# A flow-matching layer on one core: the modulation's loads kept one half tile behind, the gates' minimum split off, eight scalings moved to ScalarE

## The chip, the cores and the metric

The kernel runs on one core of a Trainium2 chip. The metric is the device time of one execution in microseconds (us), lower is better; the time of a kernel is the median of its runs. A core has five engines, each with an instruction queue of its own: TensorE (PE in the profile; its weight loads are PEld), VectorE (DVE), ScalarE (ACT), GpSimd (POOL) and SyncE (SP, which here only issues DMA transfers). They work on SBUF, 128 partitions of on-chip memory, and TensorE writes its sums into PSUM, eight banks of 128x512 fp32.

## The reference

One layer of a backbone: 512 latent tokens `x` and 256 context tokens `ctx`, width 2048, everything in fp32.

```python
mx = silu(c) @ w_mod + b_mod                      # 6 x 2048: shifts, scales and gates
sh1, sc1, gt1, sh2, sc2, gt2 = split(mx, 6)
hx = rmsnorm(x, norm1_g) * (1 + sc1) + sh1        # the context likewise, with c_ctx
q, k, v, g, lf, lb, cb, cc, cx = split_proj(hx @ w_in)
la_f = log_sigmoid(lf @ w_gate_f + b_gate_f) / 16  # la_b likewise: per-channel forget gates
o = gla_bidir(q, k, v, la_f, la_b, s_f, s_b)       # 4 heads, from the context's final states
mix = concat(rmsnorm(o) * gla_g * silu(g), cb * conv_w3(cc * cx)) @ w_out
x = x + gt1 * mix
h2 = rmsnorm(x, norm2_g) * (1 + sc2) + sh2
x = x + gt2 * ((silu(h2 @ w_ffn_gate) * (h2 @ w_ffn_up)) @ w_ffn_down)   # hidden width 5632
return rmsnorm(x, final_g)
```

Three pieces matter here. The vectors gt1, sh2, sc2 and gt2 are four of the six parts of `silu(c) @ w_mod`, 64 rows of 128 numbers, each a dot product of length 2048. The forget gates are log-sigmoids, computed as min(z, 0) - ln(1 + exp(-|z|)). The second norm's output h2 is a scale and a shift per channel of the transposed activations.

## The kernel before

**Products.** Each fp32 product is three TensorE products of a faster type: an operand is cast into a high part (`whi`, by ScalarE, line 106), and the remainder (`wlo`, by VectorE, line 107) is its low part; `mm3` then does low by high, high by low and high by high. Weights come as pieces of 128x1024 (512 KB) that SP's queue loads (line 122) into a ring of four tiles named "raw"; whi and wlo have rings of three. A projection unit is one such piece: 8 times 3 matmuls of 128x512.

**The program's stages**, in order of time: first norm and the projections of k and v (to about 290 us); the context's gates and final states, woven with the projections of q of heads 0 and 1 (to about 342); the latent gates, woven with a g projection and the first conv unit (to 412); four heads of the linear attention, woven with the remaining projections (to about 760); the output product; the FFN's up and gate products, which follow a scheme of seven half-sized products per pair instead of eight; the FFN's down products; the last norm.

**Banks.** In the stages up to the heads, PSUM is five banks of a tag "g" (`bank`) and three of a tag "a" (`abank`). Projections accumulate in "a".

**The modulation.** The dot products with w_mod are spread over the stages from 290 to 754 us. `mod_some` (lines 379 to 405) is called once per woven step (`weave`, line 564) and takes on average 1.84 half tiles of 128x1024 of w_mod: it issues the load of one and lets VectorE multiply it with silu(c) and sum it (line 405, named CUSTOM_DVE_ANT_0 in the trace and ISA in the order). There are three ways, chosen by `behind[0]`. Where it is 0, as up to the heads, the load goes through SP's queue into the ring "raw" (`load_raw`), and the reduce is issued at once. Where it is 2, as in the heads (line 705), the reduce comes two half tiles later, and the load goes through POOL's queue: two of three into tiles of their own ("wm", line 393), the third into the ring "raw" (line 397). Ahead of such a load POOL copies one column of the newest cast weight into the tile (lines 392 and 396), which ties the load's time to that cast.

**The gates.** For a group of 128 tokens, `gate_rows` does two products of 33 rows into two banks, `pzs`, one per direction. `log_gates` (lines 489 to 497) takes them: ScalarE does |z| from the banks (line 493), then one exp and one ln over both (494, 495; each has a load of its function table ahead of it), and VectorE takes min(z, 0) from the banks and subtracts the logarithm in one instruction (497). The tile `lg` between them exists once. `do_gates` does this for four groups, with one bank of "g" and one of "a".

**The second norm.** `norm2_scale` scales the rows; `norm2_back` transposes them back on TensorE, 128x256 at a time, and applies scale and shift from PSUM: the even pieces on ScalarE (line 983), the odd ones on VectorE (line 980). The first half of the tokens (hf = 0) is done while the output product runs, the second (hf = 1) inside the first column group of the FFN.

**Order.** A scheduler sets each engine's order from the order of the code and the dependencies, except SP's from the output product on, which follows the code. Each engine works in that order, so an instruction that waits holds up those behind it.

Of the kernel before, what the change touches and what calls it, by code (L numbers as in the profile page):

```python
# [11 lines left out]
ALU = mybir.AluOpType  # L12
# [41 lines left out]
def tile_hybrid_block(  # L54
# [6 lines left out]
    nc = tc.nc  # L61
# [16 lines left out]
    def big(dtype=F32):  # L78
        return xpool.tile([P, SEQ], dtype, tag="t", name="big")

    def hbig(dtype=F32, name="hbig"):
        return xpool.tile([P, SEQ], dtype, tag="h", name=name, bufs=32)

    def bank(name="bank"):
        return pspool.tile([P, 512], F32, tag="g", name=name, bufs=5)

    def abank(name="abank"):
        return pspool.tile([P, 512], F32, tag="a", name=name, bufs=3)
# [4 lines left out]
    def mm(o, l, r, start, stop):  # L93
        nc.tensor.matmul(o, l, r, start=start, stop=stop, skip_group_check=True)  # L94
# [24 lines left out]
    def load_raw(src):  # L119
        n = src.shape[-1]  # L120
        r = wpool.tile([P, 1024], F32, tag="raw", name="raw", bufs=4)
        nc.sync.dma_start(r[:, :n], src)
        return r[:, :n]
# [11 lines left out]
    def tok(t, tt):  # L135
        return t[:, tt * P : tt * P + P]
# [200 lines left out]
    def gate_rows(pz, half, d, a):  # L337

        q = slice(64 * half, 64 * half + 33)
        mm(pz, lfT[q, a : a + P], gatet[q, d, :], True, True)  # L340
# [6 lines left out]
    for i in range(KD):  # L347
# [4 lines left out]
        if i % 4 == 3:  # L352
            pcs = mod_cols(wsh, i - 3, 4)
            for c in range(4):
                nc.vector.tensor_scalar(shs[:, i - 3 + c, 0:2], pcs[:, 2 * c : 2 * c + 2], col(C_BMOD + i - 3 + c),
                                        None, op0=ALU.add)
# [19 lines left out]
    nmod, owed = [0], [0.0]  # L376

    pend, behind, unit = [], [0], []

    def mod_some(n, last):  # L380


        owed[0] += 2 * n
        while owed[0] >= 1 and (pend or nmod[0] < 2 * last):
            owed[0] -= 1
            if nmod[0] < 2 * last:
                j, hf = divmod(nmod[0], 2)
                src = wm2[j][:, hf * 1024 : hf * 1024 + 1024]
                if behind[0] and nmod[0] % 3:
                    w = gp.tile([P, 1024], F32, tag="wm", name="wm", bufs=2)  # L390

                    nc.gpsimd.tensor_copy(w[:, 0:1], unit[0])
                    nc.gpsimd.dma_start(w, src)
                elif behind[0]:
                    w = wpool.tile([P, 1024], F32, tag="raw", name="raw", bufs=4)
                    nc.gpsimd.tensor_copy(w[:, 0:1], unit[0])
                    nc.gpsimd.dma_start(w, src)
                else:
                    w = load_raw(src)
                pend.append((j, hf, w))  # L400
                nmod[0] += 1
                if len(pend) <= behind[0]:
                    continue
            j, hf, w = pend.pop(0)
            nc.vector.tensor_tensor_reduce(  # L405
                out=w, in0=w, in1=cbc[:, hf * 1024 : hf * 1024 + 1024], scale=1.0, scalar=0.0,
                op0=ALU.mult, op1=ALU.add, accum_out=modacc[:, j, hf : hf + 1])
# [81 lines left out]
    def log_gates(pool, tag, pzs, las):  # L489

        t = pool.tile([P, 2, 512], F32, tag=tag, name="lg")
        for i in range(2):
            nc.scalar.activation(t[:, i, :], pzs[i], AF.Abs)
        nc.scalar.activation(t, t, AF.Exp, scale=-1.0)
        nc.scalar.activation(t, t, AF.Ln, bias=onecol)
        for i in range(2):
            nc.vector.scalar_tensor_tensor(las[i], pzs[i], 0.0, t[:, i, :], op0=ALU.min, op1=ALU.subtract)

    def proj_units(acc, wsrc, x, units=(0, 1), part=ALL):

        for n, u in enumerate(units):
            w = load_w(wsrc[u], 8)
            unit[:] = [w[0][:, 0, 0:1].bitcast(F32)]
            for k in range(8):
                mm3(acc[:, part], sl(w, ALL, k), sl(x[8 * u + k], ALL, part), n == 0 and k == 0, n == 1 and k == 7)
            yield
# [5 lines left out]
    def do_q(h):  # L512
        acc = abank("acc")
        yield from proj_units(acc, wq[h], hx)
        q_t[h] = big()
        nc.scalar.activation(q_t[h], acc, AF.Copy, scale=QSCALE)

    def do_ctx():
        kds = [[], []]
        las = []  # L520
        for d in range(2):
            pzs = [bank("pzs") for _ in range(NCT)]
            for tt in range(NCT):
                gate_rows(pzs[tt], tt, d, SEQ + tt * P)
            las.append([big() for _ in range(NCT)])
            log_gates(hcpool, "lg", pzs, las[d])
            yield
        for d in range(2):
            for tt in range(NCT):
                pz = bank("pz")  # L530
                whole = tt == d
                mm(pz, cstt[:, B_SUFF + d, :], las[d][tt], True, not whole)
                if whole:
                    mm(pz, one16, las[d][1 - tt], False, True)
                tag, bufs = (("sq0", 2), (("lfs", "tm")[tt], 1))[d]
                e = hcpool.tile([P, 512], F32, tag=tag, name="kdc", bufs=bufs)
                nc.scalar.activation(e, pz, AF.Exp)
                nc.vector.tensor_tensor(e, e, kc[tt], op=ALU.mult)
                kds[d].append(e)
            yield  # L540
        S0[:] = [xpool.tile([P, 2, DV], F32, tag="t", name="s0") for h in range(HEADS)]
        for d in range(2):
            for hp in range(2):
                pz = bank("pz")
                for hh in range(2):
                    h = 2 * hp + hh
                    for tt in range(NCT):
                        mm(pz[:, hh * DV : hh * DV + DV], tok(kds[d][tt], h), vc[tt][hp][:, hh * DV : hh * DV + DV],
                           hh == 0 and tt == 0, tt == 1)
                for hh in range(2):  # L550
                    nc.any.tensor_copy(S0[2 * hp + hh][:, d, :], pz[:, hh * DV : hh * DV + DV])
            yield
# [11 lines left out]
    def weave(stages, fill):  # L564

        for _ in stages:
            next(fill, None)
            mod_some(MOD_STEP, 64)
        for _ in fill:
            mod_some(MOD_STEP, 64)  # L570

    weave(do_ctx(), (None for g in (do_q(0), do_q(1)) for _ in g))


    msk = []
    for d in range(2):
        t = hbig()
        nc.gpsimd.memset(t, 0.0)
        msk.append(t)
    las = [[hbig() for tt in range(NX)] for d in range(2)]  # L580

    def do_gates():
        for tt in range(NX):
            pzs = [bank("pzs"), abank("pzs")]
            for d in range(2):
                gate_rows(pzs[d], d, d, tt * P)
            log_gates(hcpool, "lg", pzs, [las[0][tt], las[1][tt]])
            yield
# [92 lines left out]
    def do_conv(c):  # L681
# [17 lines left out]
        mix[8 + c] = y  # L699

    weave(do_gates(), (None for g in (do_g(0), do_conv(0)) for _ in g))
    es_hc.close()
    es_g = ExitStack()
    gp = es_g.enter_context(tc.tile_pool(name="gp", bufs=1, side="right"))
    behind[0] = 2
    for h in range(HEADS):
# [3 lines left out]
        if h + 2 < HEADS:  # L710
            fill.insert(0, do_q(h + 2))
        weave(do_gla(h), (None for g in fill for _ in g))
    mod_some(128, 64)
    mod_finish(0, 64)
    nc.vector.tensor_scalar(gsc2, modv[:, 32:48], 1.0, None, op0=ALU.add)
# [19 lines left out]
    def bank8(name="bank8"):  # L735
        return ps2.tile([P, 512], F32, tag="b", name=name)

    def row2k(name):
        return fpool.tile([P, NB], F32, tag="e", name=name, bufs=17)
# [226 lines left out]
    def norm2_back(hf, units):  # L966
        for u in units:
            pt = bank8("pt")
            dst = row2k("h2") if hf else big()
            dst = dst.rearrange("p (k t) -> p k t", k=2)  # L970
            for kk in range(2):
                k = 2 * u + kk
                for t in range(2):
                    nc.tensor.transpose(pt[:, (2 * kk + t) * P : (2 * kk + t) * P + P],
                                        xs[2 * hf + t, k // 4][:, k % 4 * P : k % 4 * P + P], ident)
            for kk in range(2):
                k = 2 * u + kk
                src = pt[:, kk * HALF : kk * HALF + HALF]
                if kk:
                    nc.vector.tensor_scalar(dst[:, kk, :], src, gsc2[:, k : k + 1], modv[:, 16 + k : 17 + k],  # L980
                                            op0=ALU.mult, op1=ALU.add)
                else:
                    nc.scalar.activation(dst[:, kk, :], src, AF.Identity, scale=gsc2[:, k : k + 1],
                                         bias=modv[:, 16 + k : 17 + k])
            raws[hf, u] = dst
# [364 lines left out]
```

## Time and profile before

| | |
|---|---|
| median of 3 runs | 2287.91 us (2285.56 to 2290.13) |
| profiled execution | 2285.08 us |
| its span on the core | 2283.3 us |
| mean granted clock of TensorE | 0.996 |
| TensorE busy | 2233.8 us (98%) |
| VectorE busy | 1657.4 us (73%) |
| ScalarE busy | 1003.3 us (44%) |
| POOL busy | 248.4 us (11%) |

The profile is one execution. The span is the time from the first to the last instruction; the device time of the same execution is 1.8 us longer. Matmuls are pipelined: one of 128x512 takes 0.39 us in a row of the timeline but the next starts 0.2265 us after it. A row of waits names the engine, the tile and line that waited, and after the arrow what came last of the things it waited for.

### The profile page before, as it was taken

How to read it: one execution, taken by the hardware profiler on the slowest of the kernel's cores; microseconds unless marked ns; L12 is line 12 of the kernel's file. 1: busy time of each engine (PE TensorE's matmuls, PEld its weight loads, DVE VectorE, ACT ScalarE, POOL GpSimd, SP SyncE). 2: the span in 40 equal slices, each digit the busy share in tenths (PEclk: the TensorE clock that was granted, in tenths of full speed). 3: DMA queues.
4: the chain of work that ended last, by engine and by line, in shares of the span. 5: the costliest groups of instructions: out<-in, count | busy, mean ns of one | idle time of the engine just before them, and what ended most of it. 6: DMA issues, size and time to landing. Idle time of an engine off the chain costs nothing.

```text
span 2283.3 us, 28033 instructions
## 1 busy us (share of the span) xinstructions
PE 2233.8 (98%) x10276; PEld 1785.8 (78%) x10276; DVE 1657.4 (73%) x2069; ACT 1003.3 (44%) x1354; POOL 248.4 (11%) x396
## 2 busy tenths in 40 slices
PE   8999998999999999999999999999999999999997
PEld 4765666887788887777888888888888888888886
DVE  3566165565768646899788779878887887787885
ACT  3423155333233434665554455444545544433343
POOL 2433100222323000100000000000000000000000
PEclk9999999999999999999999999999999999999999
DMA  9683466565677354523643454354335596756752
GB/s 328 218 278 132 148 220 199 197 223 203 239 238 254 117 191 168 204 74 122 210 148 117 160 179 157 130 171 165 136 139 205 203 338 208 242 198 203 258 168 100
DMA packets 163410, 433.16 MB, mean 190 GB/s; under 512 B 18022, under 2 KB 38790, under 8 KB 163144
## 3 DMA queue, kind: packets, MB, share of 16 engines
q1 hardware_dynamic: 128984, 331.20, 43.4%
q0 software_dynamic: 22416, 78.66, 9.8%
q10 hardware_dynamic: 11872, 21.52, 2.5%
q8 instruction: 81, 1.33, 0.2%
q14 instruction: 57, 0.47, 0.1%
HBM read 380.95 MB, written 50.35 MB: 189 GB/s over the span
## 4 chain that ended last, share of the span: by engine, by line
issue 56%; POOL 2%; PE 1%; DVE 1%; ACT 0%; DMA 0%; POOLq 0%; DVEq 0%; ACTq 0%
POOL opd L1070 2%; PE acc L94 1%; DVE wlo L107 0%; DVE ch L849 0%; ACT y L1217 0%; DMA out<-g 0%; DVE u L1023 0%; POOL xnd L1026 0%; ACT whi L106 0%; POOL hbig L962 0%; DVE hbig L1024 0%; DVE u L869 0%; POOLq L1070 0%; ACT acc L1208 0%; DVE g L1205 0%
## 5 line engine op out<-in xcount | busy, mean ns | idle before, releaser
L106 ACT CAST whi<-ch 128x1024 fp32r<-128x1024 f32 x335 | 353.1, 1055 | 407.5 <-PE acc L94 343.3
L107 DVE TENSOR_TENSOR wlo<-ch,whi 128x1024 fp32r<-128x1024 f32 x335 | 407.6, 1221 | 122.7 <-ACT whi L106 121.9
L106 ACT CAST whi<-raw 128x1024 fp32r<-128x1024 f32 x258 | 271.0, 1052 | 455.9 <-PE acc L94 287.9
L107 DVE TENSOR_TENSOR wlo<-raw,whi 128x1024 fp32r<-128x1024 f32 x258 | 316.2, 1226 | 197.6 <-ACT whi L106 191.6
L94 PE MATMUL acc<-hhl,whi 128*128 128x512 f32 x640 | 199.1, 392 | 0.0
L94 PE MATMUL acc<-hhi,wlo 128*128 128x512 f32 x320 | 133.0, 417 | 11.8 <-DVE wlo L107 5.6
L94 PEld LDWEIGHTS acc<-hhl,whi 128*128 128x128 f32 x640 | 120.2, 188 | 27.3 <-issue 2.5
L1070 POOL DMA_DIRECT2D opd<-ol x80 | 43.3, 541 | 880.2 <-DVE ol L107 880.0
L405 DVE CUSTOM_DVE_ANT_0 wm<-wm,cbc 128x1024 f32<-128x1024 f32 x66 | 80.6, 1224 | 79.4 <-DMA wm<-wm 78.5
L94 PE MATMUL acc<-wlo,a6h 128*128 128x512 f32 (+1 forms) x330 | 127.4, 386 | 1.2 <-DVE wlo L107 1.2
L94 PE MATMUL acc<-wlo,a0h 128*128 128x512 f32 x324 | 127.5, 394 | 0.8 <-DVE wlo L107 0.8
L94 PE MATMUL acc<-whi,a6l 128*128 128x512 f32 (+1 forms) x330 | 127.1, 387 | 0.3 <-DVE v L869 0.3
L94 PE MATMUL acc<-whi,a6h 128*128 128x512 f32 (+1 forms) x330 | 127.2, 386 | 0.0
L94 PE MATMUL acc<-hhl,wlo 128*128 128x512 f32 x320 | 126.5, 395 | 0.0
L94 PE MATMUL acc<-whi,a5h 128*128 128x512 f32 x324 | 126.3, 390 | 0.0
L94 PE MATMUL acc<-hlo,whi 128*128 128x512 f32 x320 | 126.1, 394 | 0.2 <-DVE hlo L112 0.2
L94 PE MATMUL acc<-whi,a0h 128*128 128x512 f32 x324 | 126.2, 390 | 0.0
L94 PE MATMUL acc<-whi,a5l 128*128 128x512 f32 x324 | 126.2, 389 | 0.0
L94 PE MATMUL acc<-wlo,a5h 128*128 128x512 f32 x324 | 126.1, 389 | 0.0
L94 PE MATMUL acc<-whi,a0l 128*128 128x512 f32 x324 | 126.0, 390 | 0.0
L94 PE MATMUL acc<-hhi,whi 128*128 128x512 f32 x320 | 125.7, 393 | 0.0
L405 DVE CUSTOM_DVE_ANT_0 raw<-raw,cbc 128x1024 f32<-128x1024 f32 x62 | 75.4, 1222 | 49.0 <-DMA raw<-wm 48.8
(334 smaller groups left out, 4986.0 us busy)
## 6 DMA issues: line engine op xcount, KB each, us to landing
raw<-wu SPq DMA_DIRECT2D x92, 512.0 KB, 4.3
ch<-wu SPq DMA_DIRECT2D x88, 512.0 KB, 3.8
wm<-wm POOLq DMA_DIRECT2D x66, 512.0 KB, 5.4
raw<-wd SPq DMA_DIRECT2D x50, 512.0 KB, 5.8
raw<-wc SPq DMA_DIRECT2D x48, 512.0 KB, 4.9
opd<-oh ACTq DMA_DIRECT2D x80, 256.0 KB, 3.5
opd<-ol POOLq DMA_DIRECT2D x80, 256.0 KB, 3.9
ch<-wd SPq DMA_DIRECT2D x38, 512.0 KB, 4.3
```

Source lines behind the costliest of these rows:

```text
L94: nc.tensor.matmul(o, l, r, start=start, stop=stop, skip_group_check=True)
L106: nc.scalar.copy(hi, src)
L107: (eng or nc.vector).tensor_tensor(lo, src, hi, op=ALU.subtract)
L405: nc.vector.tensor_tensor_reduce(out=w, in0=w, in1=cbc[:, hf * 1024 : hf * 1024 + 1024], scale=1.0, scalar=0.0, op0=ALU.mult, op1=ALU.add, ...
L1070: nc.gpsimd.dma_start(opd[j][i, 1].rearrange("p k t -> p (k t)"), lo.bitcast(F32))
```

## The change

Three edits. First, `behind[0]` is 1 from the context's states on: the half tiles of w_mod of that stage and of the gates now go through POOL's queue, all of them into the ring "raw" (the condition for the separate tiles is now `behind[0] > 1`), each with the copy of a column ahead of it, and each is reduced one half tile later. Second, `log_gates` takes the minimum right after |z|, as a VectorE instruction of its own from the bank into the result's tile, and subtracts the logarithm there later; `do_gates` takes both banks from the tag "g". Third, for the second half of the tokens, ScalarE applies scale and shift to the odd pieces too.

```diff
@@ mod_some
-                if behind[0] and nmod[0] % 3:
+                if behind[0] > 1 and nmod[0] % 3:
                     w = gp.tile([P, 1024], F32, tag="wm", name="wm", bufs=2)
 
                     nc.gpsimd.tensor_copy(w[:, 0:1], unit[0])
@@ log_gates
         t = pool.tile([P, 2, 512], F32, tag=tag, name="lg")
+
         for i in range(2):
             nc.scalar.activation(t[:, i, :], pzs[i], AF.Abs)
+            nc.vector.tensor_scalar(las[i], pzs[i], 0.0, None, op0=ALU.min)
         nc.scalar.activation(t, t, AF.Exp, scale=-1.0)
         nc.scalar.activation(t, t, AF.Ln, bias=onecol)
         for i in range(2):
-            nc.vector.scalar_tensor_tensor(las[i], pzs[i], 0.0, t[:, i, :], op0=ALU.min, op1=ALU.subtract)
+            nc.vector.tensor_tensor(las[i], las[i], t[:, i, :], op=ALU.subtract)
@@ after weave
+    behind[0] = 1
     weave(do_ctx(), (None for g in (do_q(0), do_q(1)) for _ in g))
@@ do_gates
-            pzs = [bank("pzs"), abank("pzs")]
+            pzs = [bank("pzs") for _ in range(2)]
@@ norm2_back
-                if kk:
+                if kk and not hf:
                     nc.vector.tensor_scalar(dst[:, kk, :], src, gsc2[:, k : k + 1], modv[:, 16 + k : 17 + k],
                                             op0=ALU.mult, op1=ALU.add)
                 else:
```

The order of the engines differs in two places, about 290 to 412 us and about 980 to 1080 us. Numbers behind a name tell tiles of one name apart; they are not the same in the two kernels.

VectorE at the first latent gate stage, before: four reduces (each with a row that reads the sum) stand ahead of line 497.

```order
L405 ISA raw_2870,modacc_76<-raw_2870,cbc_79 128x1024
L405 ISA modacc_76 128x1
L405 ISA raw_2906,modacc_76<-raw_2906,cbc_79 128x1024
...
L405 ISA raw_2909,modacc_76<-raw_2909,cbc_79 128x1024
...
L497 SCALAR_TENSOR_TENSOR hbig_2676<-pzs_2684,lg_2688 128x512
L497 SCALAR_TENSOR_TENSOR hbig_2680<-pzs_2685,lg_2688 128x512
L107 TENSOR_TENSOR wlo_2840<-raw_2837,whi_2839 128x1024
```

The same stage now (line 495 is the minimum, line 499 the subtract):

```order
L553 COPY s0_2636<-pz_2664 128x256
L405 ISA raw_2793,modacc_76<-raw_2793,cbc_79 128x1024
...
L107 TENSOR_TENSOR wlo_2816<-raw_2813,whi_2815 128x1024
L495 TENSOR_SCALAR hbig_2690<-pzs_2698 128x512
L405 ISA raw_2843,modacc_76<-raw_2843,cbc_79 128x1024
...
L495 TENSOR_SCALAR hbig_2694<-pzs_2699 128x512
L405 ISA raw_2847,modacc_76<-raw_2847,cbc_79 128x1024
...
L499 TENSOR_TENSOR hbig_2690<-hbig_2690,lg_2702 128x512
L499 TENSOR_TENSOR hbig_2694<-hbig_2694,lg_2702 128x512
L107 TENSOR_TENSOR wlo_2867<-raw_2864,whi_2866 128x1024
```

The minima stand between reduces, and nothing after them reads the banks.

VectorE at the last gate stage and the conv's first pieces, now:

```order
L107 TENSOR_TENSOR wlo_2946<-raw_2943,whi_2945 128x1024
L499 TENSOR_TENSOR hbig_2693<-hbig_2693,lg_2855 128x512
L499 TENSOR_TENSOR hbig_2697<-hbig_2697,lg_2855 128x512
L405 ISA raw_2939,modacc_76<-raw_2939,cbc_79 128x1024
...
L405 ISA raw_2973,modacc_76<-raw_2973,cbc_79 128x1024
...
L405 ISA raw_2977,modacc_76<-raw_2977,cbc_79 128x1024
...
L107 TENSOR_TENSOR wlo_2987<-raw_2984,whi_2986 128x1024
L405 ISA raw_3014,modacc_76<-raw_3014,cbc_79 128x1024
...
L107 TENSOR_TENSOR wlo_3021<-raw_3018,whi_3020 128x1024
```

Each remainder of a weight stands behind reduces of half tiles that the copies of POOL tie to the cast of the weight before.

ScalarE at the second half of the norm, before:

```order
L983 ACTIVATE h2_7567<-pt_7566,modv_77,gsc2_78 128x256
L983 ACTIVATE h2_7575<-pt_7574,modv_77,gsc2_78 128x256
L983 ACTIVATE h2_7601<-pt_7600,modv_77,gsc2_78 128x256
L983 ACTIVATE h2_7609<-pt_7608,modv_77,gsc2_78 128x256
L106 CAST whi_7709<-ch_7428 128x1024
L106 CAST whi_7736<-ch_7452 128x1024
L106 CAST a1h_7616<-s_7618 128x512
```

And now:

```order
L986 ACTIVATE h2_7608<-pt_7607,modv_77,gsc2_78 128x256 x2
L986 ACTIVATE h2_7616<-pt_7615,modv_77,gsc2_78 128x256 x2
L986 ACTIVATE h2_7642<-pt_7641,modv_77,gsc2_78 128x256 x2
L986 ACTIVATE h2_7650<-pt_7649,modv_77,gsc2_78 128x256 x2
...
L106 CAST a1h_7657<-s_7659 128x512
...
L986 ACTIVATE h2_7690<-pt_7689,modv_77,gsc2_78 128x256 x2
L106 CAST whi_7750<-ch_7469 128x1024
```

The first two casts of the weights that come next (whi_7709 and whi_7736) stood behind four scalings; now the first (whi_7750) stands behind twelve, and the second, further down, behind all sixteen.

## The prediction

> **What bounds the kernel now.** I read the page's first part, then TensorE's waits, then the timeline around the two longest of them, then the ends of what they wait for.
>
> ```profile
> PE 2233.8 (98%) x10276; PEld 1785.8 (78%) x10276; DVE 1657.4 (73%) x2069; ACT 1003.3 (44%) x1354; POOL 248.4 (11%) x396
> ...
> PE acc L94 <- DVE wlo L107: 10.4, 11, 2.9
> ...
> PE acc L94 <- DVE hbig L497: 5.5, 1, 5.5
> ...
> PE pzs L94 <- DVE hbig L497: 2.4, 1, 2.4
> ```
>
> TensorE is busy in 2233.8 of 2283.3 us, so 49.5 us can be won at most. Its longest single wait (engine, tile and line, then what it waits for; us in total, times, longest) is 5.5 us, for line 497, the last step of the gates. A second one, 2.4 us, waits for the same line. The timeline shows both in one place (start, duration, engine, line, tiles; in brackets the idle time ahead of it and what ended it).
>
> ```profile
> 346.72 1.15 ACT L495 ACTIVATE lg<-lg,cidt 128x1024 f32<-128x1024 f32 x1
> ...
> 353.17 1.23 DVE L405 CUSTOM_DVE_ANT_0 raw<-raw,cbc 128x1024 f32<-128x1024 f32 x1 [2.50 <-DMA raw<-wm]
> ...
> 354.76 1.12 PE L94 MATMUL pzs<-gatet,lfT 33*128 33x512 f32 x2
> 355.76 1.22 DVE L405 CUSTOM_DVE_ANT_0 raw<-raw,cbc 128x1024 f32<-128x1024 f32 x1 [1.36 <-DMA raw<-wm]
> 356.91 1.28 DVE L497 SCALAR_TENSOR_TENSOR hbig<-pzs,lg 128x512 f32<-128x512 f32 x2
> 358.25 1.90 PE L94 MATMUL pzs<-gatet,lfT 33*128 33x512 f32 x2 [2.37 <-DVE hbig L497]
> 358.31 1.08 ACT L493 ACTIVATE lg<-pzs 128x512 f32<-128x512 f32 x2 [9.14 <-DVE hbig L497]
> ...
> 364.25 1.29 DVE L497 SCALAR_TENSOR_TENSOR hbig<-pzs,lg 128x512 f32<-128x512 f32 x2 [2.17 <-ACT lg L495]
> 365.60 0.79 PE L94 MATMUL acc<-hhi,wlo 128*128 128x512 f32 x1 [5.45 <-DVE hbig L497]
> ...
> 368.32 0.57 PE L94 MATMUL acc<-hhi,wlo 128*128 128x512 f32 x1
> ...
> 355.00:360.00 5.00, 2.63 (x4) 0.39 (x3) 3.57 (x5) 1.67 (x3) 0.00 (x0) 0.85 0.68 207
> 360.00:365.00 5.00, 0.15 (x1) 0.00 (x0) 1.98 (x4) 4.94 (x5) 0.00 (x0) 0.50 0.59 206
> 365.00:370.00 5.00, 4.40 (x13) 3.52 (x14) 1.68 (x3) 4.96 (x7) 0.00 (x0) 0.63 0.35 113
> ```
>
> The first stage's logarithm is ready at 346.72 + 1.15 = 347.9, and line 497 starts at 356.91: ahead of it in VectorE's queue stand reduces (line 405) that wait for loads of w_mod (2.50 and 1.36 us idle). Line 497 is the last reader of the banks, so the gate products of the next stage, and then everything behind them on TensorE, wait for it. The last three rows (stretch, length, busy of PE, PEld, DVE, ACT, POOL, granted clock, DMA share, GB/s) show the price: TensorE almost still from 357 to 365.6, a clock of 0.50, and 0.63 after it.
>
> **What the gates part removes.** Idle 2.37 + 5.45 = 7.8 us. The two gate products took 1.90, where the pair at 354.76 took 1.12: 0.8 more. From 365.60 to 368.32 lie six starts of matmuls, 0.45 us apart, where 24 matmuls of a unit at full clock take 5.44 us, 0.2265 each: 1.4 us. Together 9.9 us. With the minimum taken right after the product, a bank is free after Abs (0.54) and a minimum of the kind of line 497 (0.68) at most, not after the whole chain of 7.3 us from 358.31 to 365.5. I count the 9.9 as gone. Kept in full, by a minimum that stands behind a late reduce as in the order printed above, is the other end.
>
> **What the one-behind part adds.** From 290 to 412 us some 30 half tiles leave SP's queue for POOL's. Each now costs a POOL copy out of the newest cast, a POOL issue, and a reduce one half tile later.
>
> ```profile
> L405 DVE CUSTOM_DVE_ANT_0 raw<-raw,cbc x30: 1215/1224/1229, 293.6 to 409.8; 128x1024 f32<-128x1024 f32 x30
> L107 DVE TENSOR_TENSOR wlo<-raw,whi x16: 1214/1222/1226, 284.5 to 402.4; 128x1024 fp32r<-128x1024 f32 x16
> L106 ACT CAST whi<-raw x16: 1036/1050/1062, 290.2 to 406.8; 128x1024 fp32r<-128x1024 f32 x16
> ...
> L396 POOL COPY raw<-whi x33: 177/191/1268, 403.6 to 754.0; 128x1 f32<-128x1 f32 x33
> ...
> DMA to landing us min/median/max: 4.0/5.9/8.9
> ...
> raw<-wm SPq DMA_DIRECT2D x29, 512.0 KB, 4.8
> raw<-wq SPq DMA_DIRECT2D x6, 512.0 KB, 4.1
> raw<-wc SPq DMA_DIRECT2D x6, 512.0 KB, 4.3
> ...
> raw<-wm POOLq DMA_DIRECT2D x1, 512.0 KB, 4.7
> ...
> DVE raw L405 <- DMA raw<-wm: 24.7, 12, 4.2
> ```
>
> (First rows: count, then least, median and largest ns, first and last start. The landing row is that of POOL's loads into the ring, line 397, in the heads' stage; the rows below it are the loads of 285 to 410 us, SP's and one of POOL's, with the median to landing. The last row is this stretch's wait of the reduces for their loads now.) Weight loads and half tiles share the ring of four. With about two half tiles per weight unit, a weight's load takes the place of a half tile of two units before. So there is a circle over two units: cast of a unit, copy, POOL load, reduce, load of the weight two units on, its cast: 0.19 + 5.0 + 1.22 + 4.3 + 1.05 = 11.8 us, or 5.9 per unit, where TensorE wants one each 5.44. Sixteen units in this stretch lose 16 x 0.45 = 7 us. For POOL's load I take 5.0, between its least (4.0) and its median (5.9) of the busier stage. With 4.0 and SP's 4.1 the circle is 10.6, under 10.88: nothing is lost. With 5.9 and 4.8 it is 13.2, or 6.6 per unit: 18 us.
>
> VectorE's order adds to it. In the conv's piece of the order above, wlo_2987 stands behind the reduces of raw_2973 and raw_2977, which are fetched only after whi_2945 is cast. From the end of that cast: two copies 0.4, landing at 5.4, two reduces to 7.8, wlo to 9.1. The unit before, whose wlo ends at 1.3 at the earliest, has TensorE busy to 6.8. That is a hole of up to 2.3 us; before, the reduce in that place waited for a load that nothing tied to the cast. Walking the whole new order with these durations, four units are met so (holes of 2.1, 2.8, 0.3, 3.1), and the context's state products lose 0.8: 9.1 us, within the ring's bounds of 0 and 18. The ring and the queue are the same late loads, so I take 9.1 once.
>
> A hole costs more than itself when the clock falls. These rows weigh it:
>
> ```profile
> 905.00:910.00 5.00, 3.17 (x13) 2.02 (x12) 2.59 (x3) 4.02 (x5) 0.00 (x0) 1.00 0.01 5
> ...
> 1000.00:1005.00 5.00, 2.81 (x10) 1.99 (x9) 5.00 (x8) 2.66 (x4) 0.00 (x0) 0.86 0.00 0
> 1005.00:1010.00 5.00, 5.00 (x19) 3.98 (x19) 4.46 (x6) 2.66 (x4) 0.00 (x0) 0.80 0.00 0
> ...
> 1003.44 0.69 PE L94 MATMUL acc<-whi,a1l 128*128 128x512 f32 x1 [2.19 <-DVE a1l L107]
> ```
>
> 1.83 us without work at 905 kept the clock at 1.00; 2.19 us at 1001 brought 0.86 and 0.80, and 9 slow matmuls, about 1.8 us. Of my holes two or three reach that length: 0 to 5.4 us more; I take 0.9, half of one. The Trainium skill (TensorE: Matmul & The Clock Gate, "What's actually happening") has the gate fall after an idle window of about 3.4 us; by that none of the new holes would slow anything, and the term would be 0. The row at 1001 does not agree: the clock fell after less.
>
> The twelve more VectorE instructions (six calls, two minima each, 0.68 at most; the subtract takes the place of line 497 at about the same size) are 8 us of VectorE in a stretch where it stands idle 24.7 us for loads: nothing for TensorE, and inside the walk. The 29 copies are 0.19 each on POOL, which does nothing (0.00) in the three stretches above: nothing. The Trainium skill (SBUF — State Buffer, "SBUF: two separate sides") says that VectorE with two SBUF inputs and GpSimd share a pair of ports which one holds for a whole instruction; the copies' 177 to 1268 ns agree, the largest being one reduce long. It could delay a load by up to 1.1 us, which lies in the ring's bounds.
>
> Gates together: -9.9 + 9.1 + 0.9 = 0.1, call it 0. Ends: -9.9, and +8 to +14.
>
> **The second half.** Eight scalings of 128x256 leave VectorE and go to ScalarE.
>
> ```profile
> L980 DVE TENSOR_SCALAR h<-pt,gsc,modv x8: 532/534/544, 989.2 to 999.9; 128x256 f32<-128x256 f32 x8
> L983 ACT ACTIVATE h<-pt,modv,gsc x8: 547/556/569, 988.4 to 999.3; 128x256 f32<-128x256 f32 x8
> ...
> 990.00:995.00 5.00, 5.00 (x29) 4.20 (x28) 4.93 (x9) 3.79 (x7) 0.00 (x0) 1.00 0.01 2
> ...
> 1025.00:1030.00 5.00, 3.94 (x17) 2.95 (x17) 5.00 (x7) 3.56 (x4) 0.00 (x0) 1.00 0.22 90
> ...
> 995.47 0.48 PE L94 MATMUL acc<-whi,a1l 128*128 128x512 f32 x1
> ...
> 990.17 2.19 ACT L106 CAST whi<-ch 128x1024 fp32r<-128x1024 f32 x2
> ...
> 1045.00:1050.00 5.00, 4.05 (x16) 2.56 (x15) 4.97 (x8) 2.09 (x3) 0.00 (x0) 1.00 0.34 90
> 1050.00:1055.00 5.00, 4.43 (x20) 3.34 (x19) 4.94 (x6) 3.01 (x3) 0.00 (x0) 1.00 0.49 156
> ```
>
> VectorE loses 8 x 0.534 = 4.3 us, ScalarE gains 8 x 0.556 = 4.4. VectorE is full in all these stretches, and TensorE stands 1.06 + 0.95 + 0.57 us in the last three of them: with their neighbours about 2.9 us that 4.3 us less of VectorE can give back. Against it: in the new order the casts that stood at 990.17 are behind eleven or twelve scalings instead of four; at 0.5 each that is about 4 us later (994.7), their wlo ends near 997.4, and TensorE, which wants it near 995.5, waits 1.3 to 2 us, then once more at the second cast, some 2.6. The wait of 2.19 at 1003.44, with its slow 1.8, is then already spent, since a1l comes no later than it does now. Later casts cost +4, the old hole with its slowness gives -4, the relieved VectorE -2.9, of which I take 2. This part: -2, between -3.5 and +2.
>
> ```profile
> 410.00:770.00 360.00, 352.51 (x1668) 294.46 (x1667) 244.99 (x419) 121.70 (x202) 95.06 (x194) 1.00 0.66 224
> ```
>
> **Sum.** The heads' stage, whose order is the same and where TensorE is busy in 352.5 of 360 us, and the FFN I leave at 0. Span 2283.3 + 0 - 2 = 2281.3; the profiled execution of before took 2285.08, 1.8 above its span, and lies 2.8 below the median of 2287.91. So 2287.9 - 2 = 2286.
>
> **Rivals.** B, the gate's stall goes and nothing replaces it: POOL's loads land in 4.0 to 4.3 as SP's do, the circle fits under 10.88. For it: POOL's least is 4.0, and its load into the ring at this stretch's end landed in 4.7; SP's queue carries 29 loads less. Against: the later median of 5.9. 2287.9 - 7 to -10 - 2 = 2279, between 2274 and 2283. C, slower: the reduces that wait for POOL's loads hold up wlo in VectorE's queue, from the point where POOL's landing and SP's together pass 9.6 us (then 16 units lose 0.6 each, the 9.9 that is won). At 5.5 and 4.8, 16 x 0.9 = 14, plus two slow restarts of 1.8, less 9.9, less 2: +6, so 2294, between 2292 and 2299. For it: the 24.7 us which reduces wait already, and the median of 5.9. Against: the heads' stage has bigger traffic. D, the change does not do what it says in the second half: ScalarE becomes what wlo waits for, and later casts cost +4 to +5 with nothing given back, while the gates give 0: 2291. For it: eight more scalings are 4.4 us, and the slice from 990 has 1.2 free on ScalarE; against: the two from 1000 have 2.3 each.
>
> **How the numbers follow.** Forecast A (2286; its own range 2282 to 2291) 0.42, B 0.30, C 0.22, D 0.06. About 0.2%, 4.6 us, is what can be told from no change: faster is below 2283.3, slower above 2292.5. Faster: 0.12 of A and 0.95 of B, 0.34. Slower: 0.06 of A, 0.85 of C, 0.3 of D, 0.23. Within: 0.43. The range reaches into B to 2277 and into C to 2295; a third of B and of C is left out.
>
> **What would show it.** Right: no wait of TensorE on the gate's subtract, no clock of 0.50 near 360; in its place several waits of 1 to 3 us on wlo between 335 and 412, each with a reduce that ended its own wait for a POOL load just ahead of it on VectorE; the first transpose of the heads (now at 412.0) within 3 us of that. For B it comes before 406, for C after 417. In the second half the hole near 1001 splits into two near 996 and 1001, and 1025 to 1055 loses its gaps. Wrong would be a POOL landing in 290 to 412 far from 5.0, a first gate stage that itself comes late (its minima stand behind reduces), or a shift in the heads' stage, where I expect none.

## The result and the profile after

The changed kernel is slower: 2305.53 us median (2300.94 to 2307.96, 4 runs), beside 2288.97 for the kernel before on the same chip; the ratio is 1.0081, with a 95% interval of 1.0065 to 1.0097. The profiled execution has a span of 2306.0 us, 22.7 longer than that of before.

The waits of TensorE, the changed kernel (engine, tile and line, what it waited for; us in total, times, longest):

```profile
PE acc L94 <- DVE wlo L107: 24.2, 13, 5.0
...
PE po L94 <- ACT sm L649: 5.4, 6, 1.5
PE pd L94 <- DVE hbig L635: 3.9, 3, 1.7
```

The two waits for the gates (5.5 and 2.4 us before) are gone, and no row on the new minimum or subtract has come. In their place the wait for wlo has risen from 10.4 to 24.2 us. The stretches that were almost empty before are full, and others have emptied (length, busy of PE, PEld, DVE, ACT, POOL, granted clock, DMA share, GB/s):

```profile
355.00:360.00 5.00, 5.00 (x22) 3.31 (x21) 3.10 (x6) 2.21 (x3) 2.14 (x4) 1.00 0.44 168
360.00:365.00 5.00, 5.00 (x23) 3.78 (x23) 3.42 (x5) 3.75 (x5) 0.00 (x0) 1.00 0.84 301
380.00:385.00 5.00, 2.71 (x7) 2.14 (x8) 4.06 (x6) 4.94 (x5) 0.69 (x2) 0.78 0.64 188
410.00:415.00 5.00, 1.96 (x5) 1.57 (x6) 2.95 (x5) 0.00 (x0) 2.24 (x3) 0.51 0.44 118
435.00:440.00 5.00, 0.76 (x4) 0.34 (x3) 4.41 (x9) 0.13 (x1) 0.00 (x0) 1.00 0.16 60
440.00:445.00 5.00, 5.00 (x16) 3.92 (x16) 5.00 (x12) 3.41 (x7) 2.77 (x4) 0.66 0.18 36
455.00:460.00 5.00, 2.25 (x9) 1.26 (x8) 4.09 (x7) 0.08 (x1) 0.00 (x0) 1.00 1.01 381
```

Where the 22.7 us lie is read from landmarks that both programs pass: each head begins with four transposes of `pk`. The first and last start of these is in one row of each profile, line 594 of the kernel before and 597 of the changed one.

```profile
L594 PE MATMUL pk<-cidt,big x16: 270/272/273, 412.0 to 716.4; 128*128 128x128 f32 x16
```

```profile
L597 PE MATMUL pk<-cidt,big x16: 270/272/273, 420.5 to 734.1; 128*128 128x128 f32 x16
```

With the first gate product of the context (305.8 before, 306.4 after), the second head's `pk` (493.1, 511.2) and the first transpose after the heads (797.1, 818.7), from the same timelines:

| stretch | before | changed | difference |
|---|---|---|---|
| up to the context's first gate product | 305.8 | 306.4 | +0.6 |
| context and latent gates, first conv | 106.2 | 114.1 | +7.9 |
| first head | 81.1 | 90.7 | +9.6 |
| heads two to four | 304.0 | 307.5 | +3.5 |
| the rest | 1486.2 | 1487.3 | +1.1 |

The same program was profiled once more (e9, below): from the context's first gate product on, its stretches took 114.4, 91.6, 304.6 and 1487.4 us. So the losses of the gates' stretch and of the first head come again, and the 3.5 of heads two to four do not. In the profile of the changed kernel they stand at one place: it is 18.1 us late at the second head's `pk`, 17.7 at 760 and 22.7 at 774, after two waits of the last head (0.81 and 1.51 us, for steps of the linear attention) and slowed matmuls behind them.

The gates' stretch did win the stall: set side by side matmul by matmul, the changed kernel is 1.7 us late at 341 and 8.1 early at 361. From there it falls back, to 0.8 early at 387, 7.8 late at 416, 14.6 late at 444 and 18 late at 460. Here is the fall between 400 and 413, from the timeline of the changed kernel (POOL, ScalarE, VectorE, SP and TensorE; rows between are left out):

```profile
399.99 1.05 ACT L106 CAST whi<-raw 128x1024 fp32r<-128x1024 f32 x1 [7.85 <-DMA raw<-wc]
401.07 1.23 DVE L107 TENSOR_TENSOR wlo<-raw,whi 128x1024 fp32r<-128x1024 f32 x1 [2.70 <-ACT whi L106]
401.10 2.37 POOL L396 COPY raw<-whi 128x1 f32<-128x1 f32 x2 [7.50 <-ACT whi L106]
402.21 1.22 DVE L405 CUSTOM_DVE_ANT_0 raw<-raw,cbc 128x1024 f32<-128x1024 f32 x1
...
403.41 1.05 POOL L397 DMA_DIRECT2D raw<-wm  x2
...
409.35 1.22 DVE L405 CUSTOM_DVE_ANT_0 raw<-raw,cbc 128x1024 f32<-128x1024 f32 x1 [5.91 <-DMA raw<-wm]
...
410.62 1.23 DVE L405 CUSTOM_DVE_ANT_0 raw<-raw,cbc 128x1024 f32<-128x1024 f32 x1
...
411.77 1.22 DVE L107 TENSOR_TENSOR wlo<-raw,whi 128x1024 fp32r<-128x1024 f32 x1
...
411.88 0.33 SPq L122 DMA_DIRECT2D raw<-wq  x1
413.05 0.79 PE L94 MATMUL acc<-hhi,wlo 128*128 128x512 f32 x1 [4.96 <-DVE wlo L107]
415.75 1.05 ACT L106 CAST whi<-raw 128x1024 fp32r<-128x1024 f32 x1 [8.51 <-DMA raw<-wq]
```

This is the circle, once round. A cast ends at 401.04; two copies take 2.37 us; two loads are issued at 403.41, and the first lands 5.9 us later; two reduces follow to 411.85; only then is there a place in the ring for a weight's load (411.88), which lands at 415.65 and is cast at 415.75. From cast to cast it is 15.8 us for two units, 7.9 a unit, where TensorE needs 5.44. Beside it VectorE's wlo (411.77) has stood behind both reduces of that pair, and TensorE has stood 4.96 us. The turn is not an odd one: the casts of 375.69 and 415.75 are five units apart, 8.0 us each; the five in that place before took 5.7.

The first head begins with the arrears:

```profile
423.69 1.05 ACT L106 CAST whi<-raw 128x1024 fp32r<-128x1024 f32 x1 [6.89 <-DMA raw<-wq]
424.81 2.37 POOL L392 COPY wm<-whi 128x1 f32<-128x1 f32 x2 [6.06 <-ACT whi L106]
...
427.12 1.05 POOL L393 DMA_DIRECT2D wm<-wm  x2
...
435.56 1.23 DVE L405 CUSTOM_DVE_ANT_0 wm<-wm,cbc 128x1024 f32<-128x1024 f32 x1 [8.41 <-DMA wm<-wm]
...
438.54 1.22 DVE L107 TENSOR_TENSOR wlo<-raw,whi 128x1024 fp32r<-128x1024 f32 x1
...
439.81 0.50 PE L94 MATMUL acc<-hhi,wlo 128*128 128x512 f32 x1 [4.24 <-DVE wlo L107]
```

A late weight means a late cast, a late copy, a load issued late, a reduce that waits 8.41 us for it, and behind that reduce the next wlo and TensorE again. Three half tiles and a weight are issued between 427.1 and 428.8 here, and each lands 8.1 to 9.7 us after its issue. All of this is code of the heads, which the change does not touch.

### The profile page after: what moved, and what is told of

It reads as the page before. It is cut to its first block, busy times and chain, and to the rows that moved or that the text cites. A ratio compares the mean times of both kernels' runs of the same rounds, so it can differ in the third digit from the quotient of the medians.

```text
span 2306.0 us, 28123 instructions
## 1 busy us (share of the span) xinstructions
PE 2243.1 (97%) x10276; PEld 1791.6 (78%) x10276; DVE 1661.3 (72%) x2074; ACT 1005.7 (44%) x1361; POOL 287.8 (12%) x454
## 4 chain that ended last, share of the span: by engine, by line
issue 39%; PE 16%; DVE 2%; ACT 2%; POOL 1%; DMA 0%; POOLq 0%; DVEq 0%; ACTq 0%
PE acc L94 15%; POOL opd L1073 1%; DVE wlo L107 1%; ACT whi L106 0%; PE pt L1059 0%; ACT h L986 0%; DVE ch L852 0%; DVE u L872 0%; ACT hbig L967 0%; ACT big L967 0%; DMA raw<-wu 0%; ACT y L1220 0%; ACT big L986 0%; DVE hbig L1027 0%; DMA out<-g 0%
## 5 line engine op out<-in xcount | busy, mean ns | idle before, releaser
L106 ACT CAST whi<-ch 128x1024 fp32r<-128x1024 f32 x335 | 353.2, 1055 | 409.4 <-PE acc L94 347.3
L94 PE MATMUL acc<-hhi,wlo 128*128 128x512 f32 x320 | 134.5, 422 | 21.8 <-DVE wlo L107 21.0
```

The source lines that it names most:

```text
L106: nc.scalar.copy(hi, src)
```

## The experiments

In each comparison the kernel before ran on the same chip; its medians there were 2286.6, 2287.3, 2286.6 and 2286.8 us. Ratios are to it, with 95% intervals.

**The edits one by one.** Theory 1: the circle through the ring (cast, copy, POOL load, reduce, weight load) costs. Theory 2: the additional VectorE work of the gates costs. Theory 3: ScalarE in the second half costs.

e1_behind, the first edit alone:

```diff
-                if behind[0] and nmod[0] % 3:
+                if behind[0] > 1 and nmod[0] % 3:
...
+    behind[0] = 1
     weave(do_ctx(), (None for g in (do_q(0), do_q(1)) for _ in g))
```

> Only the first edit: half tiles of w_mod one behind through POOL's queue from the context's states on; gates and second norm as before. Theory 1 (the circle cast, POOL copy, POOL load, reduce, weight load is what costs): at least the changed kernel's loss, and the old gate stall stays or moves, so 2303 to 2320 us, with TensorE waiting over 15 us for wlo between 285 and 460 us. Theory 2 (the twelve more VectorE instructions and the fuller tag of banks cost): 2280 to 2292. Theory 3 (ScalarE in the second half costs): 2280 to 2292.

e2_gates, the second alone:

```diff
+            nc.vector.tensor_scalar(las[i], pzs[i], 0.0, None, op0=ALU.min)
...
-            nc.vector.scalar_tensor_tensor(las[i], pzs[i], 0.0, t[:, i, :], op0=ALU.min, op1=ALU.subtract)
+            nc.vector.tensor_tensor(las[i], las[i], t[:, i, :], op=ALU.subtract)
...
-            pzs = [bank("pzs"), abank("pzs")]
+            pzs = [bank("pzs") for _ in range(2)]
```

> Only the second edit: the minimum taken at once and both gate banks from one tag; loads of w_mod stay on SP's queue. Theory 1: the stall of 9.9 us at the latent gates goes and little takes its place, 2277 to 2284 us. Theory 2: 2295 to 2306. Theory 3: as theory 1.

e3_norm, the third alone:

```diff
-                if kk:
+                if kk and not hf:
```

> Only the third edit: the second half's odd pieces scaled by ScalarE. Theory 1: between -2 and +2 us against before, so 2287 to 2291 beside a before of 2289. Theory 2: the same. Theory 3: 2295 or more.

Measured: e1 2298.72 us, 1.0055 (1.0036 to 1.0074); e2 2280.52, 0.9976 (0.9962 to 0.9990); e3 2286.07, 0.9997 (0.9986 to 1.0008). So the first edit costs 12 us, the second wins 6, the third does nothing that can be told. As explanations of the loss, theories 2 and 3 fall. e1 is 4.3 us below the range that theory 1 gave, and its waits for wlo are 14.7 us in the whole program, where over 15 were expected in a part of it. The waits of TensorE in e1, its first four rows but the one on the program's first loads:

```profile
PE acc L94 <- DVE wlo L107: 14.7, 11, 5.5
...
PE acc L94 <- DVE hbig L497: 5.3, 1, 5.3
PE po L94 <- ACT sm L647: 2.9, 4, 1.5
PE pzs L94 <- DVE hbig L497: 2.2, 1, 2.2
```

The gate's stall stands there as it did, with the circle's loss beside it: half tiles one behind do not move line 497 forward.

**What of the first edit costs.** e4 takes the copies away, so that a load is tied to no cast; e8 keeps them, but from a column of constants; e7 keeps the reduce one behind and sends the loads through SP's queue; e11 ties them to the cast before the newest. All four have the other two edits, as the changed kernel has.

e4_no_copy:

```diff
                     w = wpool.tile([P, 1024], F32, tag="raw", name="raw", bufs=4)
-                    nc.gpsimd.tensor_copy(w[:, 0:1], unit[0])
+                    if behind[0] > 1:
+                        nc.gpsimd.tensor_copy(w[:, 0:1], unit[0])
```

> The changed kernel without POOL's copy of a cast column ahead of the loads up to the heads' stage: a load of w_mod starts when its place in the ring is free, no longer after the newest cast. Theory 1 (the tie to the cast closes the circle): loads start up to 11 us earlier, the waits for wlo between 285 and 445 us fall from 18 us to under 6, time 2283 to 2292 us. Rival 1b (POOL's slower loads or the reduce one half tile later cost by themselves, tied or not): 2300 to 2307 as the changed kernel.

e8_const_copy:

```diff
-                    nc.gpsimd.tensor_copy(w[:, 0:1], unit[0])
+                    nc.gpsimd.tensor_copy(w[:, 0:1], unit[0] if behind[0] > 1 else onecol)
```

> The changed kernel with POOL's copy kept but taken from a column that is always there, so the load is not tied to the cast while the copy still takes its turn at SBUF. If the tie costs: as the kernel without copies, 2286 to 2294 us. If the copies themselves cost (they lasted 1.2 us where they met VectorE): 2299 to 2308 us.

e7_sp_one_behind:

```diff
-                elif behind[0]:
+                elif behind[0] > 1:
                     w = wpool.tile([P, 1024], F32, tag="raw", name="raw", bufs=4)
...
                 else:
                     w = load_raw(src)
```

> The changed kernel with the reduce one half tile behind, but its loads through SP's queue in program order as before (no POOL copy, no POOL load up to the heads). If the path through POOL and its tie to the cast is what costs: 2278 to 2286 us. If reducing one half tile later, which keeps a place of the ring longer, costs by itself: 2292 or more.

e11_older_tie (`unit` now holds the last two casts):

```diff
-            unit[:] = [w[0][:, 0, 0:1].bitcast(F32)]
+            unit[:] = unit[-1:] + [w[0][:, 0, 0:1].bitcast(F32)]
...
-                    nc.gpsimd.tensor_copy(w[:, 0:1], unit[0])
+                    nc.gpsimd.tensor_copy(w[:, 0:1], unit[0 if behind[0] == 1 else -1])
```

> The changed kernel, where the copy up to the heads' stage takes its column from the cast before the newest: the tie stays, but the circle has one unit more time, about 12 us for three units of 5.44. If the circle costs: 2286 to 2294 us, like the kernels whose loads aren't tied. If the tie costs because of what POOL's copies and queue do, whichever cast they wait for: 2299 to 2306.

Measured: e4 2289.93, 1.0016 (1.0002 to 1.0030); e8 2290.53, 1.0012 (0.9997 to 1.0026); e11 2290.59, 1.0018 (1.0003 to 1.0034); e7 2281.30, 0.9971 (0.9960 to 0.9983). Beside e11, on the same chip, the changed kernel took 2309.51 (e9, below). One unit more of time in the circle is worth as much as no tie at all, 19 us there. The copy as such costs nothing that can be told: with and without it the untied kernels agree within 1 us. Nor does the reduce one half tile later, as long as SP loads: e7 and the two other edits alone (e5, same chip, 2279.6) are 1.7 us apart by medians, and their intervals overlap.

What is left is some 9 us between e8 and e7, POOL's loads without the tie. 5.8 of them lie in the gates' stretch (107.8 against 102.0 us), and one place of it can be read in e8's timeline:

```profile
339.71 5.29 SPq L122 DMA_DIRECT2D raw<-wg  x2
...
341.79 1.12 PE L94 MATMUL pzs<-gatet,lfT 33*128 33x512 f32 x2
...
344.74 1.04 ACT L106 CAST whi<-raw 128x1024 fp32r<-128x1024 f32 x1 [7.34 <-DVE modacc L405]
345.69 1.45 ACT L553 COPY s<-pz 128x256 f32<-128x256 f32 x4
...
346.51 2.07 PE L94 MATMUL pzs<-gatet,lfT 33*128 33x512 f32 x2 [3.60 <-ACT s L553]
```

And from the waits of SP's queue between 334 and 346 us:

```profile
SPq L122 <- DVE wlo L107: 9.5, 1, 9.5
```

The second pair of gate products waits 3.60 us for a bank that ScalarE empties (line 553), and ScalarE stood idle 7.34 us ahead of a cast. The cast's row names a reduce, which ended in the moment (344.64) in which the weight's load landed. That load was issued only at 339.71, after SP's queue had waited 9.5 us for a place in the ring, which a wlo freed. So the ring is short there even without the tie. That this is what the 9 us are is not tested.

**Half the load.** e12_half_load is the changed kernel with other rates:

```diff
-            mod_some(MOD_STEP, 64)
+            mod_some(0.46 if behind[0] == 1 else 1.06, 64)
```

> The changed kernel with half the half tiles per step up to the heads' stage (0.92 a unit for 1.84) and the rest in the heads (2.12 a unit). With one half tile or less for a weight, a weight's load takes the place of a weight, not of a late half tile. If the ring's circle costs: from the first context gate product to the heads 99 to 103 us (114 in the changed kernel), first head 80 to 86 us (91), time 2280 to 2290 us. If the cost goes with the number of half tiles through POOL: 106 to 109 us and 2292 to 2300.

Measured: 2303.12 us, 1.0076 (1.0055 to 1.0097). Context, gates and conv took 94.8 us, less than in any kernel so far (106.2 before, 114.1 changed), the first head 87.5. With 0.92 half tiles for a weight instead of 1.84 the loss there is gone and more. That is below the range I had given for it. The time was missed all the same, since the first head stayed above its range and heads two to four rose to 323.6 us from 307.5: what was moved there cost more than it had cost here. That the heads can't take 15% more half tiles was not in my expectation.

**The sum.** e5_gates_norm has the second and third edit:

```diff
-    behind[0] = 1
     weave(do_ctx(), (None for g in (do_q(0), do_q(1)) for _ in g))
```

> The changed kernel without its first edit: gates' minimum and banks, and the second half on ScalarE, with the loads of w_mod left on SP's queue. If the edits add up (e2 6 us faster, e3 nothing): 2278 to 2283 us beside a before of 2286 to 2288, ratio 0.995 to 0.999. If the third edit only pays or costs together with the second: outside that.

e6_behind_gates and e10_first_two have the first and second, e9_all_three is the changed kernel again, e13_first_third has the first and third, and e14_part_third the first two with two of the third's eight pieces. e6, e10 and e14 against the changed kernel:

```diff
-                if kk and not hf:
+                if kk:                            # e6, e10
+                if kk and (not hf or u < 6):      # e14
```

> First and second edit, without the third. The edits alone gave +12, -6 and 0. If they added up: 2290 to 2295 us. If the first edit costs more once the gate's stall is gone, since the stall was also time in which late loads caught up: 2300 to 2308, as the changed kernel. If the third edit is the partner that costs: 2290 to 2295 too, and e5 slow.

> The changed kernel once more, beside the next one on the same chip: it was 17 us slower than before, first and second edit without the third 12 us. If the third edit costs in their company: 5 us or more above the next one again. If that was the scatter of few runs: within 3 us of it, both 11 to 18 us above before.

> First and second edit, without the third, beside the one above. Third edit free: 2298 to 2306 us, within 3 us of it. Third edit costs there: 2297 to 2301 and the other 2303 or more.

> First and third edit, without the second. The first alone took 2298.7 us. If the third edit costs in the first's company (all three were 11 us above the first two on one chip, though the two programs are alike up to 980 us): 2304 us or more. If the 11 us need the second too, or belong to that one build: 2296 to 2302.

> First and second edit, and the third for the last two of its eight pieces only. If the third edit's work costs: a quarter of 11 us above the first two, 2300 to 2303. If it costs nothing: 2296 to 2301. If the 11 us belong to a build and not to its work: anything from 2296 to 2312, without relation to the number of pieces.

The last two columns are each from one profiled execution, which lies up to 8 us from the median (e5 2271.9, e13 2309.7).

| kernel | edits | us, median | ratio | gates' stretch | first head |
|---|---|---|---|---|---|
| e2 | 2 | 2280.5 | 0.9976 (0.9962, 0.9990) | 101.5 | 83.9 |
| e3 | 3 | 2286.1 | 0.9997 (0.9986, 1.0008) | 107.3 | 79.9 |
| e5 | 2, 3 | 2279.6 | 0.9954 (0.9939, 0.9970) | 99.7 | 80.2 |
| e1 | 1 | 2298.7 | 1.0055 (1.0036, 1.0074) | 109.0 | 93.0 |
| e13 | 1, 3 | 2301.4 | 1.0061 (1.0038, 1.0083) | 110.0 | 94.3 |
| e6 | 1, 2 | 2299.2 | 1.0046 (1.0032, 1.0059) | 113.1 | 90.1 |
| e10 | 1, 2 | 2298.6 | 1.0056 (1.0039, 1.0074) | 112.4 | 88.9 |
| e14 | 1, 2, part of 3 | 2303.9 | 1.0069 (1.0046, 1.0093) | 114.4 | 89.8 |
| changed | 1, 2, 3 | 2305.5 | 1.0081 (1.0065, 1.0097) | 114.1 | 90.7 |
| e9 | 1, 2, 3 | 2309.5 | 1.0092 (1.0066, 1.0119) | 114.4 | 91.6 |

Two things follow. The first and second edit don't add up (12 - 6 = 6, measured 12): with the circle closed, taking the stall away wins nothing. (e6 came 0.8 us below the range that I had given for this case.) The gates' stretch is 109 to 110 us with the stall and 112 to 115 without, while without the first edit it falls from 106 and 107 to 100 and 102. And all three are above the first two by 9 us on average (2305.5 and 2309.5 against 2299.2 and 2298.6). The third edit's own work isn't what costs there: from the first transpose after the heads to the end of the span it is 1487.3 us in the changed kernel and 1486.2 in e6, and up to about 980 us the two programs have the same order. e13 (between 2291 and 2310 in six runs) doesn't show it clearly, e14 lies between. These kernels scatter widely, e9 over 19 us and e5 over 10. In the profiled executions of these four, 4 to 5 us of it lie in heads two to four and 1.2 behind them. What carries the 9 us stays open.

e5 is the fastest kernel here by its median, 7.7 us below before, 10.5 as the ratio has it, and clear of it. Of e2, e7 and e15 it is not clear. Its first wait rows:

```profile
PE acc L94 <- DVE wlo L107: 9.7, 9, 3.2
...
PE po L94 <- ACT sm L647: 3.8, 3, 2.0
```

**The tie in the heads.** There POOL's copies are tied to the newest cast in all kernels so far. e15 has e5's edits and e11's first line, with every copy from the older cast; e16 has e12's rates in addition.

```diff
-            unit[:] = [w[0][:, 0, 0:1].bitcast(F32)]
+            unit[:] = unit[-1:] + [w[0][:, 0, 0:1].bitcast(F32)]
...
-            mod_some(MOD_STEP, 64)                       # e16
+            mod_some(1.06 if behind[0] else 0.46, 64)    # e16
```

> Second and third edit (2279.6 us before), and in the heads' stage POOL's copy takes its column from the cast before the newest. If the tie to the newest cast costs TensorE there too: up to the 6 us that it stands in that stage, 2273 to 2278. If what it waits for there is not tied loads: 2278 to 2282. If loads that start earlier get in the way of weights: 2283 or more.

> As the kernel just above, with 0.92 half tiles per unit up to the heads and 2.12 in them. The gates' stage took 95 us with this rate in place of 100, but the heads 316 in place of 302 when tied to the newest cast. If it was the tie that made the heads slow: heads 300 to 306 us, 2270 to 2277. If it is the number of half tiles: heads 310 or more, 2285 to 2295.

Measured: e15 2281.48, 0.9973 (0.9961 to 0.9984), no better than e5; e16 2296.92, 1.0052 (1.0035 to 1.0069), with 94.7 us for the gates' stretch and 418 for the heads, against 386 in e15. e16's profiled execution is the slowest of its eight, 2309.8; from the medians and the gates' stretches I estimate that its heads cost some 20 us more than e15's, not the 33 of the profiles. So in the heads the tie costs nothing that can be told at the old rate, where two of three half tiles have places of their own. It is the number of half tiles that they can't take more of, tied or not.

## Why the prediction was wrong

Two steps failed. The largest error is the heads' stage, which I left at 0 since its order is the same: it lost 13.1 us. The second is the size of the circle and of the clock behind it, 9.1 and 0.9 us in my sum, about 14 and 3.7 in the gates' stretch. The 22.7 us of the profiles are 7.9 there (9.9 won, 17.8 lost), 13.1 in the heads, and 1.7 before and behind.

**The gates' stall, -9.9: right.** e2 is 9.9 us early at 369, and no wait of TensorE for the last step of the gates is left in it or in the changed kernel. But even with SP's loads e2 keeps only 4.8 of it at 410: TensorE's waits for wlo in that stretch, none before, are 4.5 us. So the stall had hidden waits for late weights.

**The circle, +9.1 within 0 to 18: the right mechanism, mis-sized.** The stretch rose by 7.9 with 9.9 won, so it lost 17.8. TensorE's waits in it are 13.1 us, 11.6 of them for wlo, and matmuls slowed after two of them make 3.7 (below), so the circle's own share is about 14. POOL's loads landed in 5.3 us and SP's in 4.0 to 4.6, within what I had put in:

```profile
raw<-wm POOLq DMA_DIRECT2D x30, 512.0 KB, 5.3
raw<-wq SPq DMA_DIRECT2D x6, 512.0 KB, 4.0
raw<-wc SPq DMA_DIRECT2D x6, 512.0 KB, 4.2
```

With these the sum 0.19 + 5.3 + 1.22 + 4.1 + 1.05 is 11.9, and the circle above took 15.8. Two terms were too small in this turn. I took one reduce, where the place that the weight waits for is freed by the second: 1.25 more. And I took one copy of 0.19; there are two in a row, and started in the moment when VectorE starts on the same cast they lasted 2.37 together, each as long as the wlo (1.23) and the reduce (1.22) beside it. I had the rule for that before me, the Trainium skill (SBUF — State Buffer, "SBUF: two separate sides"), and put it aside as a possible 1.1 us of delay. The trace agrees with it at this place. It does not meet every turn: of the 29 copies up to the heads 9 took over 0.9 us, and in e8, whose copies there wait for no cast, 6 of 29. So the copies explain this turn and not the sixteen units; how much each term adds over all turns was not measured. Outside the circle the same copies cost nothing (e8).

**The heads at 0: wrong, +13.** I argued from an unchanged order, and named a shift in the heads as a sign of being wrong. The order was the same, but the stage starts with weights in arrears, and each late cast there makes the next loads late. The traces of all runs show the arrears at one weight, the first of the next head's g projection: its cast begins 0.2 us after the first `pk` transpose in every kernel without the tie up to the heads, and in e12, and 2.2 to 7.2 us after it in all tied ones at the old rate, e11 (2.2) among them. The first head takes 89 to 94 us in these and 80 to 85 in the untied ones. In the changed kernel its 9.6 us are the wait of 4.24 at 440, 1.7 of slowed matmuls behind it, and waits of 1.71 and 1.51 at 458 and 460 for steps of the linear attention. That the arrears are the cause is argued from these rows; no run changes them alone. The 3.5 us of the other heads did not come again in e9.

**The clock, +0.9 within 0 to 5.4: mis-sized.** After the holes of 3.39 us at 382, 4.96 at 413 and 4.24 at 440 the matmuls fell back a further 1.7, 1.9 and 1.7 us, 5.4 together, with clocks of 0.78, 0.51 and 0.66 in the stretches shown above. That is the 1.8 which the hole at 1001 had shown, three times: the upper end. The first two are part of the gates' 17.8, the third of the first head's 9.6. The window of about 3.4 us of the Trainium skill (TensorE: Matmul & The Clock Gate, "What's actually happening") is reached or passed by all three, so they agree with it. The rows at 1020 and 1055 below do not, as the row at 1001 did not: after waits of 1.85 and 1.88 us the clock was 0.71 and 0.80. A wait's length alone does not tell it either, since at 905 the clock stayed at 1.00 with 1.83 us without work.

**VectorE's twelve instructions and POOL's copies as mere work, 0: right** (e2, e8).

**The second half, -2 within -3.5 and +2: the later casts right, the gain not seen.** In the changed kernel's rows the casts come later (the wait now stands on whi), the gaps further on (1025 to 1055 before, some 22 us later now) have closed, and a new one has opened at 1055:

```profile
1022.82 0.73 PE L94 MATMUL acc<-whi,a1l 128*128 128x512 f32 x2 [1.85 <-ACT whi L106]
```

```profile
1020.00:1025.00 5.00, 2.63 (x10) 1.55 (x9) 4.76 (x7) 5.00 (x10) 0.00 (x0) 0.95 0.00 0
1025.00:1030.00 5.00, 5.00 (x17) 3.96 (x17) 3.76 (x5) 2.26 (x3) 0.00 (x0) 0.71 0.01 2
...
1050.00:1055.00 5.00, 5.00 (x23) 3.92 (x22) 4.94 (x7) 3.67 (x5) 0.00 (x0) 1.00 0.51 160
1055.00:1060.00 5.00, 3.12 (x11) 2.20 (x11) 5.00 (x9) 1.59 (x3) 0.00 (x0) 0.86 0.08 32
1060.00:1065.00 5.00, 5.00 (x19) 3.98 (x19) 3.36 (x5) 2.12 (x4) 0.00 (x0) 0.80 0.68 188
1065.00:1070.00 5.00, 5.00 (x24) 4.14 (x23) 5.00 (x7) 3.64 (x5) 0.00 (x0) 1.00 0.59 164
1070.00:1075.00 5.00, 5.00 (x24) 4.14 (x23) 4.94 (x7) 1.57 (x2) 0.00 (x0) 1.00 0.45 174
```

Against before it loses 5.3 us (21.6 late at 1016, 26.9 at 1028) and is 21.8 late at 1085: about 0 in all. e3 gives -0.5 with an interval of -3 to +2, which leaves room for the -2.

**The rivals.** C was the case, by its own mechanism and at its place. POOL's and SP's landings together were 9.4 us, just under my deciding point of 9.6, which the second reduce alone moves down to about 8.4. Its 14 for the circle and 3.6 for slow restarts are what the gates' stretch lost; its price, 2294, was too low since it too left the heads at 0. B is what e7 shows when the loads stay on SP's queue: 2281.3, in B's range. Of what I said would show it, the waits on wlo with a late reduce ahead of them came as told, and the transposes at 420.5 are on C's side (after 417).

## What to carry to other kernels

Before a load is tied to another engine's progress, draw the whole circle that it closes: if the loaded tile gives its place to something that the tied-to work needs, then each term of the circle, and its queueing, is paid per turn, and slack in a single latency says little. A stall in front of such a circle isn't worth its length, because the circle refills it; here an edit that wins 6 us alone won nothing beside it. And a stage with an unchanged order can still inherit the arrears of its predecessor.

## What the runs showed that I had not expected

The copies of the changed kernel, all of one column (least, median and largest ns):

```profile
L396 POOL COPY raw<-whi x62: 180/198/1271, 291.9 to 776.8; 128x1 f32<-128x1 f32 x62
```

Most take 0.2 us; those that met VectorE's two-operand work in the rows above took 1.2. All are of one size, so the length depends on when a copy starts. The fastest kernel is the change without its first edit, and the gates' stretch can be had in 95 us (e12, e16) if half the half tiles go elsewhere, but the heads, with 7.5 us of 360 free on TensorE before, took more for some 15 further half tiles: 13 us in the profile of e12 beside that of the changed kernel, and by my estimate some 20 in e16 beside e15.
